# Loading order of the start, and the way one bank's operands are built, in a recurrent/attention decoder block

## The chip, the cores and the metric

The kernel runs on one core of a Trainium2 chip. A core has TensorE (PE, matrix products; its weight loads are listed as PEld), VectorE (DVE), ScalarE (ACT), GpSimd (POOL) and SyncE (SP). Every engine works through its own instructions in order. DMAs are issued here by SP and by ACT, each a queue in order: an issue that waits for a free buffer holds all issues behind it. The metric is device time in microseconds of one execution. A tile is named by its tag in the program (wraw, S, T, hf and so on), and the profile leaves buffer numbers out.

## The reference, cut to what matters

x is 2048 rows of 1024 float32 values, one layer.

```python
mod = c_act @ w_mod[l] + b_mod[l]              # c_act = silu(c), one row of 1024
shift, scale, gate = jnp.split(mod, 3, axis=-1)
h = rms_norm(x, g_norm[l]) * (1.0 + scale[:, None, :]) + shift[:, None, :]
proj = h @ w_in[l]                             # 1024 x 8192
x_rnn, z_rnn, q, k, v, z_attn, g_r, g_a = jnp.split(proj, IN_SPLITS, axis=-1)
...
x = x + gate[:, None, :] * (merged @ w_o[l])
```

Between the two parts quoted stand a recurrent branch (causal convolution, gated linear recurrence) and an attention branch with three dilated windows; both end in a product with a 1024 x 1024 matrix. The change touches only how `h` is made and how `v`, the first eighth of the projection that is computed, is multiplied out.

## The kernel before, in words

*Split products.* All large products keep float32 accuracy by splitting each operand into a high part (rounded, written by ACT: `hi_act`) and a low part (the operand minus the high part, written by POOL: `lo_pool`, or by VectorE: `lo_dve`). `mm3` (L149) then makes three matmuls: high by high, high by low, low by high.

*Banks and halves.* The 2048 positions are four banks of 512. The projection runs in two halves of two banks: `values_half(f, xs)` for the half f, then 28 Strassen products (`strassen`, L272) for all other columns of `w_in`. A Strassen product multiplies 2 x 2 blocks (the two banks by the two halves of the 1024 input channels) with seven block products instead of eight. Its right operands are the blocks of `h`: `B11` and `B21` (first bank of the half, channels 0 to 511 and 512 to 1023), `B22` (second bank, upper channels) and four block sums `T1` to `T4`. `B12` (second bank, lower channels) is needed for the values only. The seven products are taken in the order B11, T2, T3, T1, B21, T4, B22.

*The start.* Constants and the nine parameter rows are loaded by SP, transposed by PE (L462) and copied into `par` (L463). `x0`, the first bank of x, is loaded in two tiles of 1024 KB by SP (L386, `load_x`) and normalised (`norm_x`: squares on ACT, scaling on VectorE, L396). Then come four groups j of 256 channels (L478 to L501). For shift and scale each, a group loads a tile of modulation weights (1024 KB, SP, L483). VectorE sums the products of its first KV = 6 channel blocks with `ca` = silu(c) into `acc` (L485, L487); PE adds blocks 6 and 7 in one-column matmuls (`pg<-ca,T`) and folds `acc` down with `ones` (`pg<-ones,acc`). The bias goes on at L498 (`mod`), and `gs` is made at L499. Then `build_even` builds the blocks k = 2j and 2j + 1 of the first bank. When all modulation weights are loaded, `x1`, the second bank, is loaded.

*build* (L398) makes one block of 128 channels by 512 positions: four PE transposes (L403), the high part by ACT out of PSUM (L407), the full value `hf` by VectorE out of PSUM (L408), and the low part, by VectorE where k is 0, 3 or 6 and by POOL otherwise.

*Values.* `load_wv(m)` brings the value weights of two heads, m = 0 to 3: four loads of 256 KB into `wraw` (five buffers, L350), each split by ACT (L155) and POOL (L161) into tiles `S` (seven buffers, four to one m). `values` makes two groups of 48 matmuls for each m and bank, with `h` as the stationary operand and 256 columns of weights moving; `store_values` copies the result out of PSUM on ACT (L549) and stores it from SP (L551). For m = 0 of the first bank, `values_by_halves` takes the lower channels first, so that it can start before the upper blocks are built. One half has 768 value matmuls.

*build_odd* (L419) is a generator that `values_half` steps once after each group of 48 matmuls: 6 steps during the first bank's m = 1 to 3, the rest during the second bank's m = 3, 0, 1, 2, up to 14 in all. In each of its first four steps it builds block k of `B12` and of `B22` and makes block k of `T1`, `T2` and `T3` (L436 to L439, splits at L441: T1 and T3 low on VectorE, T2 low on POOL). In its next four steps it makes `T4` out of the stored high and low parts of B21 and T2 (L447, L448; low on POOL).

*What sets the order.* Outside the attention part, a planner orders the instructions of each engine by the program's order and by its own model of the times; `tc.issue_after(ins)` holds the issues of a block behind one instruction of the same engine. There are 14 buffers `T` of 8 KB a partition: x0 takes 2, B11 and B21 4, the modulation weights 8; x1, B22 and the block sums take them over as they come free.

## Time and profile before

| | us |
|---|---|
| three runs | 2361.22, 2364.11, 2366.56 (median 2364.11) |
| profiled execution | 2364.77, its span 2363.0 |
| start, 0 to 32.7 | no value matmul yet |
| values of the first half, 32.7 to 160.3 | 127.6 |
| Strassen products of the first half, 160.3 to 786.8 | 626.5 |
| values of the second half, 786.8 to 896.2 | 109.4 |
| Strassen products of the second half, attention, output | the rest, 1466.8 |

A row of a group of instructions reads: line, engine, operation, output<-input, shape, count | total busy time in us, mean of one in ns | idle time of the engine just before them, and what ended it. A row of a list in order of time reads: start, duration, engine, line, operation. A row of the waits reads: who waited <- for whom: total us, times, longest. A row of busy times by stage reads: stage, its length, then busy us (and count) of PE, PEld, DVE, ACT, POOL, then the granted clock of TensorE, the share of DMA time and GB/s.

### The profile page before, as it was taken

What the parts mean: (1) busy time and instruction counts of PE and PEld (TensorE: products, weight loads), DVE (VectorE), ACT (ScalarE), POOL (GpSimd) and SP (SyncE); (2) the same over time, 40 slices, a digit from 0 to 9 for tenths busy, and PEclk for the clock granted to TensorE, in tenths of its full rate; (3) what the DMA queues carried; (4) which work ended last, traced back from release to release, by engine and by line L of the source; (5) the groups of instructions that cost most, each with busy time, mean ns of one, the idle gap of its engine ahead of it and who ended that gap; (6) DMA issues with size and microseconds to landing.
All of it is one profiled execution on the core that took longest, in us unless ns stands there. A gap on an engine that the chain in (4) does not pass through costs nothing.

```text
span 2363.0 us, 34030 instructions
## 1 busy us (share of the span) xinstructions
PE 2232.6 (94%) x11397; PEld 1877.8 (79%) x11397; DVE 1340.2 (57%) x2423; ACT 1170.4 (50%) x2332; POOL 1003.8 (42%) x765
## 2 busy tenths in 40 slices
PE   5999999999999989999999998799999999989998
PEld 5897777777777888888888877688888898978887
DVE  6847666666575653544444462266666777645433
ACT  3436656666642434655444410366667878622111
POOL 2566656665555553433121110355445656443000
PEclk9999999999999999999999999899999999999999
DMA  7266777777788639999776776888999889797652
GB/s 266 82 207 235 267 240 259 255 248 249 251 272 251 205 120 322 326 346 314 247 243 231 222 264 212 259 262 255 300 299 273 263 248 287 217 337 275 225 178 97
DMA packets 420902, 585.44 MB, mean 248 GB/s; under 512 B 72446, under 2 KB 278518, under 8 KB 419704
## 3 DMA queue, kind: packets, MB, share of 16 engines
q1 hardware_dynamic: 383288, 463.72, 62.9%
q10 hardware_dynamic: 37440, 119.55, 13.3%
q8 instruction: 90, 1.47, 0.2%
q14 instruction: 84, 0.69, 0.1%
HBM read 367.14 MB, written 216.01 MB: 247 GB/s over the span
## 4 chain that ended last, share of the span: by engine, by line
PE 61%; DMA 12%; DVE 11%; ACT 5%; issue 5%; POOL 3%; SPq 2%; ACTq 1%; DVEq 0%; POOLq 0%
PE pj L147 43%; PE pq L147 7%; PE o L147 3%; PE sc L147 3%; PE pg L147 2%; DMA wraw<-in_w_in_dram 2%; POOL S L161 1%; PE pT L1082 1%; DMA w<-wD 1%; DVE acc L487 1%; DMA wD<-s 1%; ACT S L188 1%; DMA kraw<-qT 1%; PE pT L1095 1%; DMA qT<-t 1%
## 5 line engine op out<-in xcount | busy, mean ns | idle before, releaser
L147 PE MATMUL pj<-T,S 128*128 128x512 f32 x4704 | 1119.5, 398 | 33.7 <-DVE ev L340 15.7
L147 PEld LDWEIGHTS pj<-T,S 128*128 128x128 f32 x4704 | 887.8, 189 | 254.0 <-DVE ev L340 21.1
L147 PE MATMUL pj<-yh,w 128*128 128x512 f32 x1024 | 371.7, 408 | 11.7 <-ACT yh L155 10.4
L161 POOL TENSOR_TENSOR S<-wraw,S 128x512 fp32r<-128x512 f32 x168 | 240.7, 1444 | 175.8 <-ACT S L188 100.5
L147 PEld LDWEIGHTS pj<-yh,w 128*128 128x128 f32 x1024 | 195.6, 191 | 50.3 <-ACT yh L155 12.5
L147 PE MATMUL pj<-yl,w 128*128 128x512 f32 x512 | 204.0, 399 | 2.3 <-POOL yl L161 1.4
L998 ACT ACTIVATE pp<-pp,st 128x256 f32<-128x256 f32 (+3 forms) x256 | 133.8, 524 | 89.5 <-DVE st L997 88.7
L147 PE MATMUL pj<-S,T 128*128 128x256 f32 x1152 | 161.9, 297 | 10.3 <-POOL S L161 7.0
L147 PEld LDWEIGHTS pj<-S,T 128*128 128x128 f32 x1152 | 151.9, 202 | 12.3 <-POOL S L161 8.0
L161 POOL TENSOR_TENSOR S<-s,S 128x512 fp32r<-128x512 f32 x84 | 114.7, 1366 | 89.7 <-ACT S L188 43.7
L164 DVE TENSOR_TENSOR ptl<-pT,pth 128x384 fp32r<-128x384 f32 (+1 forms) x160 | 97.8, 628 | 60.8 <-ACT pth L155 58.6
L1062 ACT ACTIVATE pp<-pp,M 128x256 f32<-128x256 f32 (+3 forms) x256 | 118.0, 523 | 12.7 <-DVE M L1186 12.7
L642 DVE SCALAR_TENSOR_TENSOR xc<-xr,par,xc 128x512 f32<-128x512 f32 x96 | 87.0, 907 | 61.2 <-ACT xc L636 58.1
L997 DVE CUSTOM_DVE_ANT_0 pp<-sc,msk 128x256 f32<-128x256 f32 (+3 forms) x256 | 105.2, 449 | 24.6 <-PE sc L147 21.4
L294 DVE TENSOR_TENSOR u<-pj,u 128x512 f32<-128x512 f32 x56 | 38.4, 686 | 140.8 <-PE pj L147 91.1
L147 PEld LDWEIGHTS pj<-yl,w 128*128 128x128 f32 x512 | 98.1, 192 | 18.5 <-POOL yl L161 2.6
L161 POOL TENSOR_TENSOR kq<-kraw,kq 128x512 fp32r<-128x512 f32 (+1 forms) x64 | 100.4, 1578 | 19.4 <-ACT kq L155 13.9
L161 POOL TENSOR_TENSOR vh<-vraw,vh 128x256 fp32r<-128x256 f32 (+1 forms) x64 | 66.4, 1037 | 94.8 <-ACT vh L155 83.1
L161 POOL TENSOR_TENSOR wh<-vraw,wh 128x640 fp32r<-128x640 f32 (+1 forms) x32 | 48.4, 1513 | 135.2 <-ACT wh L155 74.7
L147 PE MATMUL pq<-oh,mh 128*128 128x512 f32 x256 | 98.0, 394 | 7.9 <-ACT mh L155 7.9
L147 PE MATMUL pq<-ol,mh 128*128 128x512 f32 x256 | 100.8, 394 | 0.3 <-POOL ol L161 0.3
L147 PE MATMUL pq<-oh,ml 128*128 128x512 f32 x256 | 99.6, 390 | 0.0
(290 smaller groups left out, 3886.2 us busy)
## 6 DMA issues: line engine op xcount, KB each, us to landing
sD<-S ACTq DMA_DIRECT2D x196, 512.0 KB, 3.1
S<-sD SPq DMA_DIRECT2D x196, 512.0 KB, 5.4
w<-wD SPq DMA_DIRECT2D x128, 512.0 KB, 6.2
wraw<-in_w_in_dram SPq DMA_DIRECT2D x136, 256.0 KB, 3.3
wD<-s ACTq DMA_DIRECT2D x64, 256.0 KB, 4.1
T<-in_w_mod_dram SPq DMA_DIRECT2D x8, 1024.0 KB
vN<-ev SPq DMA_DIRECT2D x64, 128.0 KB, 2.5
zaT<-ev SPq DMA_DIRECT2D x32, 256.0 KB, 2.8
```

Source lines behind the costliest of these rows:

```text
L147: last_mm[0] = nc.tensor.matmul(o, lhsT=l, rhs=r, start=st, stop=sp, **kw).ins
L161: nc.gpsimd.tensor_tensor(o, i, h.bitcast(F32), ALU.subtract)
L164: nc.vector.tensor_tensor(o, i, h.bitcast(F32), ALU.subtract)
L188: last_hi[0] = nc.scalar.activation(t[:, 0], src, AF.Copy).ins
L294: nc.vector.tensor_tensor(u2[:], Z[:], u1[:], ALU.add)
L487: nc.vector.scalar_tensor_tensor(acc[:], t[:, k, :], ca[:, k : k + 1], acc[:], ALU.mult, ALU.add)
L642: nc.vector.scalar_tensor_tensor(xc, xr[:, i : i + CH], cw(i), xc, ALU.mult, ALU.add)
L997: nc.vector.tensor_tensor_reduce(pdst, s_ps, mask, 1.0, 3e38, ALU.add, ALU.min, m_)
L998: nc.scalar.activation(pdst, pdst, AF.Exp, bias=m_, scale=-1.0, accum_out=l_)
L1062: nc.scalar.activation(pp, pp, AF.Copy, scale=w)
L1082: nc.tensor.transpose(pt[:, c0 + j * P : c0 + (j + 1) * P], pp[i][:, k * P : (k + 1) * P], ident)
L1095: nc.tensor.transpose(pt[:, c * P : (c + 1) * P], pp[:, half * P : (half + 1) * P], ident)
```

## The change

- *Start.* The two loads of `x0` are the first issues of SP. The constants are loaded by ACT's queue and the nine parameter rows by POOL's queue. Then SP loads the modulation weights of groups 0 and 1, the first half of value weights 0, groups 2 and 3, the second half of value weights 0, then `x1`, then value weights 1 (held behind x1 by `issue_after`). Before, SP loaded each group's modulation weights in the loop over the groups, and the value weights where the planner put them.
- *Modulation.* KV goes from 6 to 5: VectorE sums five channel blocks, PE takes three.
- *First bank (start only).* `hf` is made by ACT as a second pass over PSUM, and all low parts by VectorE. The first bank of the second half is built as before.
- *Second bank.* The eight blocks are built in the first four steps, with `hf` by ACT into eight buffers `hx` that are kept, and low parts on VectorE. The block sums take the next eight steps: T3 and T1 of block k in one, T2 and T4 in the next. T4 is B21 high - T2 (unsplit) + B21 low, two operations instead of three. All low parts are made by VectorE.

```diff
@@ -34,7 +34,7 @@
-KV = 6
+KV = 5
@@ -134,7 +134,6 @@
     pools = Pools()
 
     cs = T(cp, [P, N_CST_A], F32, "cs")
-    nc.sync.dma_start(cs[:], cst[:, :N_CST_A])
     ident = cs[:, K_ID : K_ID + P]
     qm = cs[:, K_QM : K_QM + 4]
     par = T(cp, [P, N_PAR], F32, "par")
@@ -189,7 +188,7 @@
         lo_pool(t[:, 1], src, t[:, 0])
         return t
 
-    pair_id, last_hi = {}, [None]
+    pair_id, last_hi, last_load = {}, [None], [None]
 
...
@@ -339,19 +338,21 @@
             else:
                 nc.vector.tensor_tensor(dst, perm(ps[:]), perm(u[:]), ALU.add)
 
+    def load_wv_half(m, k):
+
+        wh = T(wq, [P, KH, 2 * P], F32R, "S", bufs=7)
+        wl = T(wq, [P, KH, 2 * P], F32R, "S", bufs=7)
+        for k2 in range(0, KH, 2):
+            t = T(wq, [P, 2, 2 * P], F32, "wraw", bufs=NRAW)
+            rows = slice((k + k2) * P, (k + k2 + 2) * P)
+            last_load[0] = nc.sync.dma_start(
+                t[:], wcol(4 * D + m * 2 * P, 2 * P)[rows].rearrange("(k p) m -> p k m", p=P)).ins
+            hi_act(wh[:, k2 : k2 + 2], t[:])
+            lo_pool(wl[:, k2 : k2 + 2], t[:], wh[:, k2 : k2 + 2])
+        return wh, wl
+
     def load_wv(m):
-        ws = []
-        for k in range(0, KT, KH):
-            wh = T(wq, [P, KH, 2 * P], F32R, "S", bufs=7)
-            wl = T(wq, [P, KH, 2 * P], F32R, "S", bufs=7)
-            for k2 in range(0, KH, 2):
-                t = T(wq, [P, 2, 2 * P], F32, "wraw", bufs=NRAW)
-                rows = slice((k + k2) * P, (k + k2 + 2) * P)
-                nc.sync.dma_start(t[:], wcol(4 * D + m * 2 * P, 2 * P)[rows].rearrange("(k p) m -> p k m", p=P))
-                hi_act(wh[:, k2 : k2 + 2], t[:])
-                lo_pool(wl[:, k2 : k2 + 2], t[:], wh[:, k2 : k2 + 2])
-            ws.append((wh, wl))
-        return ws
+        return [load_wv_half(m, k) for k in range(0, KT, KH)]
 
...
@@ -383,7 +384,7 @@
         xs = []
         for r in range(0, 4, 2):
             t = T(pool, [P, 2, D], F32, tag, bufs=bufs)
-            nc.sync.dma_start(t[:], xv[n, r : r + 2].rearrange("r j d -> j r d"))
+            last_load[0] = nc.sync.dma_start(t[:], xv[n, r : r + 2].rearrange("r j d -> j r d")).ins
             xs += [t[:, 0, :], t[:, 1, :]]
         return xs
 
@@ -395,69 +396,79 @@
             rstd(ss)
             nc.vector.tensor_scalar(t, t, ss[:, 1:2], None, ALU.mult)
 
-    def build(st, names, xs, k):
+    def build(st, names, xs, k, first=False, keep=None):
 
         hh, hl = B[names[k // KH]]
         pt = T(pg, [P, 4, P], F32, "pg")
         for r in range(4):
             nc.tensor.transpose(pt[:, r, :], xs[r][:, k * P : (k + 1) * P], ident)
         pv = pt[:].rearrange("p r j -> p (r j)")
-        hf = T(st, [P, CH], F32, "hf", bufs=2)
         g, s = gs[:, k : k + 1], sh[:, k : k + 1]
         nc.scalar.activation(hh[:, k % KH, :], pv, AF.Identity, bias=s, scale=g)
-        nc.vector.tensor_scalar(hf[:], pv, g, s, ALU.mult, ALU.add)
-        (lo_dve if k % 3 == 0 else lo_pool)(hl[:, k % KH, :], hf[:], hh[:, k % KH, :])
-        return hf
+        if keep is not None or first:
+            hf = keep if keep is not None else T(st, [P, CH], F32, "hf", bufs=2)[:]
+            nc.scalar.activation(hf, pv, AF.Identity, bias=s, scale=g)
+            lo_dve(hl[:, k % KH, :], hf, hh[:, k % KH, :])
+        else:
+            hf = T(st, [P, CH], F32, "hf", bufs=2)
+            nc.vector.tensor_scalar(hf[:], pv, g, s, ALU.mult, ALU.add)
+            (lo_dve if k % 3 == 0 else lo_pool)(hl[:, k % KH, :], hf[:], hh[:, k % KH, :])
 
     def operand(name):
         B[name] = (slot(), slot())
 
-    def build_even(st, xs, ks=range(KT)):
+    def build_even(st, xs, ks=range(KT), first=False):
         for k in ks:
-            build(st, ("B11", "B21"), xs, k)
+            build(st, ("B11", "B21"), xs, k, first)
 
     def build_odd(st, xs):
 
         B["B12"] = (T(st, [P, KH, CH], F32R, "b12h"), T(st, [P, KH, CH], F32R, "b12l"))
-        for name in ("B22", "T1", "T2", "T3"):
-            operand(name)
+        operand("B22")
         f32 = lambda b, i, k: B[b][i][:, k, :].bitcast(F32)
         tt = nc.vector.tensor_tensor
-
-        def split(name, k, t, lo):
+        h = [T(st, [P, CH], F32, "hx", bufs=KT)[:] for _ in range(KT)]
+        for k in range(KH):
+            for k2 in (k, KH + k):
+                build(st, ("B12", "B22"), xs, k2, keep=h[k2])
+            yield
+        for name in ("T1", "T2", "T3", "T4"):
+            operand(name)
+
+        def split(name, k, t):
             hh, hl = B[name]
-            hi_act(hh[:, k, :], t[:])
-            lo(hl[:, k, :], t[:], hh[:, k, :])
+            hi_act(hh[:, k, :], t)
+            lo_dve(hl[:, k, :], t, hh[:, k, :])
 
         for k in range(KH):
-            h1 = build(st, ("B12", "B22"), xs, k)
-            h2 = build(st, ("B12", "B22"), xs, KH + k)
-            t = [T(st, [P, CH], F32, f"t{i}", bufs=1) for i in range(3)]
-            tt(t[0][:], h1[:], f32("B11", 0, k), ALU.subtract)
-            tt(t[0][:], t[0][:], f32("B11", 1, k), ALU.subtract)
-            tt(t[1][:], h2[:], t[0][:], ALU.subtract)
-            tt(t[2][:], h2[:], h1[:], ALU.subtract)
-            for i in range(3):
-                split(f"T{i + 1}", k, t[i], lo_pool if i % 2 else lo_dve)
+            h1, h2 = h[k], h[KH + k]
+            t = T(st, [P, CH], F32, "t0", bufs=2)[:]
+            tt(t, h2, h1, ALU.subtract)
+            split("T3", k, t)
+            tt(h1, h1, f32("B11", 0, k), ALU.subtract)
+            tt(h1, h1, f32("B11", 1, k), ALU.subtract)
+            split("T1", k, h1)
             yield
-        operand("T4")
-        for k in range(KH):
-            t = [T(st, [P, CH], F32, f"t{i}", bufs=1) for i in range(2)]
-            for i in range(2):
-                tt(t[i][:], f32("B21", i, k), f32("T2", i, k), ALU.subtract)
-            tt(t[0][:], t[0][:], t[1][:], ALU.add)
-            split("T4", k, t[0], lo_pool)
+            tt(h2, h2, h1, ALU.subtract)
+            split("T2", k, h2)
+            t = T(st, [P, CH], F32, "t0", bufs=2)[:]
+            tt(t, f32("B21", 0, k), h2, ALU.subtract)
+            tt(t, t, f32("B21", 1, k), ALU.add)
+            split("T4", k, t)
             yield
 
+
+    x0 = load_x(hp, 0, "T", 14)
+    nc.scalar.dma_start(cs[:], cst[:, :N_CST_A])
     prow = T(vx, [P, P], F32, "prow")
     for r0, ap in (
         (C_C, c[0]), (C_G, g_norm[0]), (C_BM, b_mod[0]), (C_BG, b_gate[0]), (C_CB, conv_b[0]), (C_LAM, lam[0]),
     ):
         n = ap.shape[0] // P
-        nc.sync.dma_start(prow[r0 : r0 + n, :], ap.rearrange("(k p) -> k p", p=P))
-    nc.sync.dma_start(prow[C_CW : C_CW + 32, :], conv_w[0].rearrange("j (k p) -> (j k) p", p=P))
-    nc.sync.dma_start(prow[C_BA : C_BA + 8, :], b_a[0])
-    nc.sync.dma_start(prow[C_BX : C_BX + 8, :], b_x[0])
+        nc.gpsimd.dma_start(prow[r0 : r0 + n, :], ap.rearrange("(k p) -> k p", p=P))
+    nc.gpsimd.dma_start(prow[C_CW : C_CW + 32, :], conv_w[0].rearrange("j (k p) -> (j k) p", p=P))
+    nc.gpsimd.dma_start(prow[C_BA : C_BA + 8, :], b_a[0])
+    nc.gpsimd.dma_start(prow[C_BX : C_BX + 8, :], b_x[0])
     pt = T(pg, [P, CH], F32, "pg")
     nc.tensor.transpose(pt[:, :N_PAR], prow[:N_PAR, :], ident[:N_PAR, :N_PAR])
     nc.vector.tensor_copy(par[:], pt[:, :N_PAR])
@@ -466,7 +477,6 @@
     nc.scalar.activation(ca[:], par[:, C_C : C_C + KT], AF.Sigmoid)
     nc.vector.tensor_tensor(ca[:], ca[:], par[:, C_C : C_C + KT], ALU.mult)
 
-    x0 = load_x(hp, 0, "T", 14)
     norm_x(vx, x0)
     operand("B11")
     operand("B21")
@@ -475,12 +485,23 @@
     mod = T(cp, [P, 2, KT], F32, "mod")
     sh = mod[:, 0, :]
     gs = T(cp, [P, KT], F32, "gs")
+    w_m, ws0 = {}, []
+
+    def load_mod(j):
+        for q in range(2):
+            w_m[q, j] = t = T(hp, [P, KT, 256], F32, "T", bufs=14)
+            c0 = q * D + j * 256
+            nc.sync.dma_start(t[:], w_mod[0, :, c0 : c0 + 256].rearrange("(k p) m -> p k m", p=P))
+
+    for j in range(4):
+        load_mod(j)
+        if j % 2:
+
+            ws0.append(load_wv_half(0, j // 2 * KH))
     for j in range(4):
         pm = T(pg, [P, 2, 2], F32, "pg")
         for q in range(2):
-            t = T(hp, [P, KT, 256], F32, "T", bufs=14)
-            c0 = q * D + j * 256
-            load = nc.sync.dma_start(t[:], w_mod[0, :, c0 : c0 + 256].rearrange("(k p) m -> p k m", p=P))
+            t = w_m[q, j]
             acc = T(vx, [P, 256], F32, "acc", bufs=2)
             nc.vector.tensor_scalar(acc[:], t[:, 0, :], ca[:, 0:1], None, ALU.mult)
             for k in range(1, KV):
@@ -498,8 +519,8 @@
         nc.vector.tensor_tensor(mod[:, :, j2], pm[:], bm[:, :, j2], ALU.add)
         nc.vector.scalar_tensor_tensor(gs[:, j2], mod[:, 1, j2], 1.0, par[:, C_G + 2 * j : C_G + 2 * j + 2],
                                        ALU.add, ALU.mult)
-        build_even(vx, x0, range(2 * j, 2 * j + 2))
-    with tc.issue_after(load.ins):
+        build_even(vx, x0, range(2 * j, 2 * j + 2), first=True)
+    with tc.issue_after(last_load[0]):
         x1 = load_x(hp, 1, "T", 14)
 
 
@@ -569,12 +590,16 @@
     def values_half(f, xs):
 
         n0, n1 = banks(f)
-        for _ in values_by_halves(vx, 0, load_wv(0), n0):
+        for _ in values_by_halves(vx, 0, load_wv(0) if f else ws0, n0):
             pass
         norm_x(vx, xs)
         odd = build_odd(vx, xs)
         for m in range(1, 4):
-            ws = load_wv(m)
+            if m == 1 and not f:
+                with tc.issue_after(last_load[0]):
+                    ws = load_wv(m)
+            else:
+                ws = load_wv(m)
             for _ in values(vx, m, ws, n0):
                 next(odd)
         for m in (3, 0, 1, 2):
```

## The prediction

> **What bounds the kernel now.** I read the page first, then busy times by stage, and inside the stages that the diff touches the order of time and the list of who waited for whom.
>
> ```profile
> span 2363.0 us, 34030 instructions
> PE 2232.6 (94%) x11397; PEld 1877.8 (79%) x11397; DVE 1340.2 (57%) x2423; ACT 1170.4 (50%) x2332; POOL 1003.8 (42%) x765
> PE 61%; DMA 12%; DVE 11%; ACT 5%; issue 5%; POOL 3%; SPq 2%; ACTq 1%; DVEq 0%; POOLq 0%
> ```
>
> ```profile
> 0.00:70.50 70.50, 41.39 (x235) 38.37 (x235) 49.20 (x126) 21.10 (x35) 17.99 (x18) 0.90 0.69 230
> 32.70:160.30 127.60, 119.14 (x897) 116.85 (x898) 87.65 (x132) 47.19 (x84) 62.76 (x44) 0.92 0.47 144
> 786.80:896.20 109.40, 100.13 (x801) 99.02 (x800) 57.00 (x79) 42.91 (x78) 59.88 (x42) 0.95 0.50 155
> ```
>
> The whole span is TensorE's: 94% busy, 61% of the chain. So a gain is only where PE idles or is slow, and the diff touches two such places: the first 160 us (start, and the values of the first half, 32.7 to 160.3), and 786.8 to 896.2 (the values of the second half). The columns after the length of a stage are PE, PEld, DVE, ACT, POOL. In the two value stages PE idles 127.6 - 119.1 = 8.5 us and 109.4 - 100.1 = 9.3 us; before 32.7 it hardly works. That is all that can be won except PE's own speed: some 24 us before the first value matmul, and 18 us in the stages.
>
> The start, in order of time (start, duration, engine; in square brackets the idle time before it and who ended it):
>
> ```profile
> 4.39 0.83 SPq L386 DMA_DIRECT2D T<-in_x_dram  x2
> 5.46 0.43 PE L462 MATMUL pg<-cs,prow 120*128 120x120 f32 x1 [5.46 <-DMA prow<-in_b_x_dram]
> 9.14 18.03 SPq L350 DMA_DIRECT2D wraw<-in_w_in_dram  x10
> 9.59 1.06 ACT L394 ACTIVATE hf<-T 128x1024 bf16<-128x1024 f32 x1 [1.61 <-DMA T<-in_x_dram]
> 15.22 0.99 PE L147 MATMUL pg<-ca,T 128*128 128x1 f32 x4 [9.33 <-DVE T L396]
> 27.21 5.40 SPq L483 DMA_DIRECT2D T<-in_w_mod_dram  x4
> 31.45 0.16 DVE L498 TENSOR_TENSOR mod<-pg,par 128x4 f32<-128x4 f32 x1 [1.96 <-PE pg L147]
> 32.73 5.95 PE L147 MATMUL pj<-S,T 128*128 128x256 f32 x24 [1.32 <-ACT T L407]
> 53.38 6.42 PE L147 MATMUL pj<-S,T 128*128 128x256 f32 x52
> 66.98 0.16 DVE L498 TENSOR_TENSOR mod<-pg,par 128x4 f32<-128x4 f32 x1 [1.56 <-PE pg L147]
> 70.50 8.75 PE L147 MATMUL pj<-S,T 128*128 128x256 f32 x63 [0.16 <-DVE T L164]
> ```
>
> SP is a queue in order. Ten value-weight loads (L350) hold it from 9.14 to 27.2, because they wait for free wraw tiles, and the modulation weights of groups 1 to 3 stand behind them. Group 0 gives its shift and scale at 31.45, group 3 at 66.98; only from 70.5 has PE both halves of the operand and streams. The two rows of value matmuls show a second thing: 24 take 5.95 us (0.248 each), 52 take 6.42 us (0.123 each). PE runs at half rate in part of the start, though the granted clock of the slice says 1.00 there.
>
> **The change part by part.**
>
> *x ahead, parameters off SP.* Ten small DMAs leave SP; x is issued at 0.74 instead of 4.39, 3.65 us earlier. x was there at 9.59, 5.2 us after its issue, so now at 5.9. The constants go to ACT's queue, one issue of some 0.4 us, beside an idle ACT: nothing. The nine parameter loads go to POOL's queue, which no DMA of this trace uses. Bounds: as on SP (nine landed by 5.46), and at POOL's nearest row, 1.3 us per instruction (the s<-wraw row below), 9 x 1.3 = 11.7, plus some 2 us to land: 14. I take 12, nearer to the upper end, since it is POOL's own row. At 12 it costs nothing: the first modulation tile cannot be there before (next step). At 14 it costs 2 us. POOL has nothing else to do before the first split of weights. Waiting for these loads are PE's first transpose and DVE's copy of the parameters; behind it on DVE stand the scaling of x and the sums.
>
> The Trainium skill, SBUF — State Buffer, section "SBUF: two separate sides", speaks against this part: descriptors of a DMA that POOL issues are written through a port pair that VectorE can hold, so such loads starve. By that rule the loads would be late by VectorE's work before they land; the scalings of x, four of 0.75 us (L396, below), are 3 us, an end of 2351 instead of 2348. No run here shows it yet, and the sum does not need it.
>
> *Modulation weights ahead of the value weights.* The rate while DMA is the limit:
>
> ```profile
> 20.00:25.00 5.00, 1.30 (x5) 0.94 (x6) 5.00 (x4) 2.78 (x5) 5.00 (x4) 1.00 0.53 169
> 35.00:40.00 5.00, 5.00 (x31) 5.00 (x31) 4.75 (x9) 0.00 (x0) 0.97 (x1) 1.00 1.10 348
> ```
>
> 348 GB/s is 3.0 us for a tile of 1024 KB. x (two tiles) is done at 8.9, group 0 at 11.9 and 14.9, group 1 at 20.9, the first half of value weights 0 at 22.4, group 2 at 28.4, group 3 at 34.4, the second half at 35.9, x of the second bank at 41.9, value weights 1 (added wait: behind that x on SP) at 44.9. The dip to 169 GB/s at 20 to 25, SP blocked, goes. Weights 1 must be split by four POOL operations (1.46 each, S<-wraw below), so are ready at 51; PE wants them some 6 us after the operand is complete, so they cost nothing unless that comes before 45.
>
> Sums of group 0, with KV = 5: L485 and four L487,
>
> ```profile
> 31.91 1.44 ACT L407 ACTIVATE T<-pg,mod,gs 128x512 fp32r<-128x512 f32 x2 [5.79 <-DVE gs L499]
> 34.16 0.68 DVE L164 TENSOR_TENSOR T<-hf,T 128x512 fp32r<-128x512 f32 x1
> 38.48 0.58 PE L147 MATMUL pg<-ca,T 128*128 128x1 f32 x4
> 39.02 2.57 DVE L487 SCALAR_TENSOR_TENSOR acc<-T,ca,acc 128x256 f32<-128x256 f32 x5
> L147 PE MATMUL pg<-ca,T 128*128 128x1 f32 x64 | 12.6, 301 | 9.7 <-DVE T L396 9.3 <-DVE mod L498 0.4
> ```
>
> 0.51 us an operation alone (five in 2.57), so 2.4 per tile. Last tile at 14.9, sums at 17.3; I add 2 for x's scaling on the same engine; then the last matmuls at 0.25 each (four in 0.99), ten of them, 2.5; then the same 1.3 us from mod (31.45) to the first value matmul (32.73). 17.3 + 2 + 2.5 + 1.3 = 23.1, and the first half of the weights, split by ACT and POOL, is there at 23.3. So PE's dense work starts at 23.5 instead of 32.7: 9.2 us earlier.
>
> From there PE's own work counts, since it was busy for 119.1 of the 127.6 us. Groups 1 to 3: with KV = 5 the 64 matmuls of ca (two instructions each) become 96, 8 per group more, 24 here, at 0.25 (slow) or 0.145 (four in 0.58): 3.5 to 6, I take 5 of cost. The 8 operations that VectorE saves are hidden work. In build, hf goes to ACT (0.72 each, two in 1.44) and the five POOL lows go to VectorE: ACT is idle at 47 of 127.6 us, nothing; VectorE gives up 0.80 (L408, below) and takes 0.68, nothing.
>
> The waits of PE in this stage, 32.6 to 160.3 (total, times, longest):
>
> ```profile
> PE pj L147 <- ACT T L407: 2.6, 2, 1.3
> PE pg L147 <- DVE acc L487: 2.5, 4, 1.4
> PE pg L403 <- DVE hf L408: 1.9, 1, 1.9
> PE pj L147 <- POOL S L161: 1.7, 1, 1.7
> ```
>
> The sums, the hf wait and the wait on POOL's S go, as tiles are no longer late and POOL has fewer lows; the wait for the built operand (2.6) stays, and some wait for weights 1 or for the norm of the second bank's x comes. 8.5 becomes 5: 3.5 gained, with -2 and 7 as ends. At last the half rate: 24 + some 45 instructions at 0.248 instead of 0.123 cost 9 us after 32.7. With no late tiles PE's stream has fewer holes; I take 3 of the 9. First half: 9.2 - 5 + 3.5 + 3 = 10.7 us.
>
> *The odd operands.* The second half has the clean picture:
>
> ```profile
> PE pj L147 <- POOL S L161: 5.3, 2, 3.0
> PE pg L403 <- DVE hf L408: 2.9, 2, 1.8
> 805.19 0.55 PE L403 MATMUL pg<-cs,T 128*128 128x128 f32 x3 [1.11 <-DVE T L396]
> L161 POOL TENSOR_TENSOR S<-wraw,S 128x512 fp32r<-128x512 f32 x23 | 33.0, 1460 | 17.6 <-PE pj L147 9.6 <-issue 4.3 <-ACT S L155 3.3
> L161 POOL TENSOR_TENSOR T<-t,T 128x512 fp32r<-128x512 f32 x8 | 12.0, 1504 | 11.7 <-ACT T L155 11.7
> L161 POOL TENSOR_TENSOR s<-wraw,s 128x512 fp32r<-128x512 f32 x4 | 5.2, 1288 | 13.9 <-DMA wD<-s 12.2 <-ACT s L155 1.7
> L164 DVE TENSOR_TENSOR T<-t,T 128x512 fp32r<-128x512 f32 x8 | 8.2, 1030 | 0.1
> L408 DVE TENSOR_SCALAR hf<-pg,gs,mod 128x512 f32<-128x512 f32 x10 | 7.9, 804 | 4.2 <-ACT b12h L407 2.2 <-POOL T L161 2.0
> L164 DVE TENSOR_TENSOR b12l<-hf,b12h 128x512 fp32r<-128x512 f32 x2 | 3.6, 1777 | 0.0
> L396 DVE TENSOR_SCALAR T<-T,ss 128x1024 f32<-128x1024 f32 x4 | 2.9, 752 | 0.1
> L155 ACT ACTIVATE T<-t 128x512 fp32r<-128x512 f32 x16 | 10.0, 631 | 30.8 <-DVE t L448 10.8 <-DVE t L437 9.7 <-DVE t L439 8.3
> ```
>
> PE waits 5.3 us for POOL's S because POOL, in order, sits in front of block-sum lows that wait for ACT (11.7 us idle). With all lows of a half's block sums and second-bank values on VectorE, POOL has only S left: the 5.3 go. The 2.9 behind hf (L403): VectorE's hf sat behind sums, ACT makes it now, and the sums come only after all eight blocks; I take half. The norm (1.1) stays. 5.3 + 1.5 less 0.8 for ACT's queue, where 8 hf more and 16 highs stand ahead of S: 6 us, ends -1 and 9.3. VectorE's own count stays: eight hf and four of the T4 subtractions go, some ten lows come. Its operations take 0.68 alone and up to 1.77 beside POOL, which is now busy 15 us less.
>
> Sum: 10.7 + 6 = 16.7. The profiled execution took 2364.8 us (span 2363.0 and 1.8 around it), the median of the three runs is 2364.1; 2364.8 - 16.7 = 2348.
>
> **The rivals.** Everything here compares with a noise of 0.2%, 4.7 us, which is what a measurement of this kernel can tell.
>
> *PE is fast in the start.* If the denser stream keeps PE at 0.123 us a matmul, the whole 9 us of half rate goes, 6 more, and the idle of both stages falls by 3 more: 2339. For it: the 52 at 0.123 come inside a long stream. Against: the 24 at 0.248 were a stream of 6 us too.
> The Trainium skill, TensorE: Matmul & The Clock Gate, Part 1, gives a rule: the array is at half clock until about 3.4 us of sustained activity. By that rule this rival holds, at 2339 where the sum by rows gives 2348. The trace agrees only in part: 5.95 us of streaming at 32.73 stayed slow to its end.
>
> *The start does not move as far.* If the parameters land only after the first tiles, or PE finishes each group's matmuls behind 24 slow value matmuls, the 9.2 shrink to 3 and the half-rate gain is nil: 2364.8 - 7.7 = 2357. For it: PE is in order, and the slice from 35 to 40 has PE busy for all of its 5.00 us.
>
> *VectorE's block sums become the bound (slower).* All lows and sums are now one row on VectorE, each low waiting for ACT's high: 48 operations at p (24 lows; six subtractions or additions for each of four k), and 24 hand-offs of 0.8 (ACT's 0.63 and the way there and back). Between the normalised x and the second Strassen product, which reads T2, there are some 98 us in the first half (an estimate: x there at 41.9, some 12 for its norm, the values' end at 149.6, 3 for the first product) and 88 in the second (18 us into the stage, by the row at 805.19, to 3 us behind an end at 103). At p = 1.77 the row is 85 + 19 = 104: 6 and 16 us late, less 16.7 gained: 2370. It is slower only from p = 1.71 on. The T<-t row above has a mean of 1.03, b12l 1.78 in two operations, and POOL, beside which the long ones stand, does less: little chance.
>
> *The gain does not come through.* The idle time moves behind the values, to the first Strassen products waiting for their weights: about 2363.
>
> **How the numbers follow.** Forecast (2342 to 2354) 0.50; fast PE 0.19; a short start 0.16; no effect 0.07; VectorE bound 0.08. The likeliest is 2348. Leaving out the worst of the slow rival and the far end of the fast one (all ends together, 9.2 + 7 + 9 - 3.5 + 9.3 = 31, give 2334): 2331 to 2361. Below 2359.4 lie the first three but for 0.01 of the short start: 0.84; slower than 2368.8: 0.08; the rest 0.08.
>
> **What would show it.** The first value matmul near 23 us and PE's stream from about 60 (now 70.5); the four mod rows about 10 us apart; L350 no longer holding SP before the modulation weights; in both value stages no PE wait on POOL S; the first Strassen matmul near 150, and the second value stage near 103 us long. Wrong would be: PE waits on DVE T or ACT T at the first Strassen products, parameter loads landing after 15 us, or PE still at 0.25 us a matmul through most of the start.

## The result, and the profile after

The changed kernel is slower: ratio to the kernel before 1.0044, 95% interval 1.003 to 1.0058 (medians 2374.46 and 2363.65 us). 2348 was forecast, with 2331 to 2361 as the range. The profiled execution took 2371.3 us (span 2369.6), 6.6 us of span more than before.

Busy times by stage of the changed kernel (stage, length, then PE, PEld, DVE, ACT, POOL, granted clock, share of DMA, GB/s); the limits are the first value matmul and the first Strassen product of each half:

```profile
0.00:53.70 53.70, 14.03 (x63) 13.29 (x63) 19.53 (x85) 15.71 (x26) 10.08 (x18) 1.00 0.81 264
53.70:175.20 121.50, 118.75 (x900) 118.43 (x901) 60.91 (x111) 58.80 (x101) 42.76 (x28) 0.96 0.35 104
175.20:800.80 625.60, 590.14 (x2492) 469.38 (x2492) 409.74 (x492) 348.90 (x579) 373.99 (x265) 0.98 0.76 257
800.80:901.70 100.90, 97.57 (x807) 96.93 (x806) 46.04 (x81) 48.95 (x87) 44.08 (x29) 0.98 0.54 167
```

Before, the start was 32.7, the first value stage 127.6, the second 109.4 (110.0 by the limits used here). So both value stages became shorter, by 6 and 9 us, and the start became 21 us longer; the Strassen products between kept their length (626.5 before, 625.6 now). The loss is all in the start. Its instructions in order of time (rows left out are marked by dots):

```profile
1.30 0.70 POOL L468 DMA_DIRECT2D prow<-in_c_dram  x1 [0.46 <-issue]
...
6.21 1.06 ACT L395 ACTIVATE hf<-T 128x1024 bf16<-128x1024 f32 x1 [3.76 <-DMA T<-in_x_dram]
7.14 0.52 POOL L471 DMA_DIRECT2D prow<-in_b_x_dram  x1 [1.55 <-DMA prow<-in_c_dram]
...
12.20 0.46 PE L473 MATMUL pg<-cs,prow 120*128 120x120 f32 x1 [12.20 <-DMA prow<-in_b_x_dram]
...
15.18 0.28 DVE L474 COPY par<-pg 128x120 f32<-128x120 f32 x1
...
21.87 1.38 ACT L154 ACTIVATE S<-wraw 128x512 fp32r<-128x512 f32 x2 [8.97 <-DMA wraw<-in_w_in_dram]
...
35.43 1.32 ACT L154 ACTIVATE S<-wraw 128x512 fp32r<-128x512 f32 x2 [12.18 <-DMA wraw<-in_w_in_dram]
36.13 2.48 POOL L160 TENSOR_TENSOR S<-wraw,S 128x512 fp32r<-128x512 f32 x2 [11.06 <-DMA wraw<-in_w_in_dram]
36.77 1.28 ACT L477 ACT_TABLE_LOAD   x1
38.06 0.21 ACT L477 ACTIVATE ca<-par 128x8 f32<-128x8 f32 x1
...
38.70 1.44 PE L146 MATMUL pg<-ca,T 128*128 128x1 f32 x6 [26.04 <-DVE ca L478]
...
53.77 1.20 PE L146 MATMUL pj<-S,T 128*128 128x256 f32 x4
```

The parameters are in `par` at 15.46 (15.18 and 0.28). The next thing that the modulation needs is one ACT operation of 0.21 us, the sigmoid of c (L477). It runs at 38.06. ACT works in order, and in its list the sigmoid stands behind the four splits of value weights 0 (L154). The second two of them wait until 35.4 for weights that the new loading order brings behind all modulation weights. PE waits 26.0 us for `ca`, with the modulation weights of all groups there or on the way. This is 22.6 us of waiting (38.06 less 15.46) for an operation whose input was ready. In the kernel before, the same operation ran right behind the copy of the parameters, ahead of every split:

```profile
6.25 0.21 ACT L466 ACTIVATE ca<-par 128x8 f32<-128x8 f32 x1 [4.24 <-DVE par L463]
```

A smaller delay stands ahead of it: PE's transpose of the parameters ends at 12.66, but VectorE copies them into `par` only at 15.18, behind the scalings of x in its own list.

The second value stage, PE's waits and the groups that the forecast spoke of:

```profile
PE pj L146 <- POOL S L160: 3.1, 2, 2.7
PE pg L404 <- DVE T L397: 0.2, 1, 0.2
L160 POOL TENSOR_TENSOR S<-wraw,S 128x512 fp32r<-128x512 f32 x23 | 36.9, 1630 | 43.3 <-PE pj L146 42.5 <-POOL T L160 0.8
L163 DVE TENSOR_TENSOR T<-hx,T 128x512 fp32r<-128x512 f32 x12 | 9.8, 818 | 0.6 <-ACT hx L410 0.6
L163 DVE TENSOR_TENSOR T<-t,T 128x512 fp32r<-128x512 f32 x8 | 6.5, 817 | 2.0 <-ACT T L154 2.0
```

PE waited 9.3 us there before (5.3, 2.9 and 1.1), now 3.3. POOL, which sat 11.7 us in front of block-sum lows, now idles in front of its splits almost only until PE has freed an S buffer (42.5 of 43.3 us). VectorE's lows take 0.82 us on average.

### The profile page after: what moved, and what is told of

The parts are those of the page before. It is cut to its first block, busy times and chain, and to the rows that moved or that the text cites. A ratio compares the mean times of both kernels' runs of the same rounds, so it can differ in the third digit from the quotient of the medians.

```text
span 2369.6 us, 34107 instructions
## 1 busy us (share of the span) xinstructions
PE 2236.5 (94%) x11429; PEld 1883.4 (79%) x11429; DVE 1303.9 (55%) x2414; ACT 1188.8 (50%) x2358; POOL 967.9 (41%) x743
## 5 line engine op out<-in xcount | busy, mean ns | idle before, releaser
L146 PE MATMUL pj<-T,S 128*128 128x512 f32 x4704 | 1122.1, 398 | 32.5 <-DVE ev L339 17.3
L160 POOL TENSOR_TENSOR S<-wraw,S 128x512 fp32r<-128x512 f32 x168 | 249.6, 1497 | 286.1 <-ACT S L187 107.5
L146 PE MATMUL pj<-S,T 128*128 128x256 f32 x1152 | 156.8, 292 | 5.9 <-POOL S L160 5.9
L160 POOL TENSOR_TENSOR S<-s,S 128x512 fp32r<-128x512 f32 x84 | 114.1, 1358 | 89.3 <-ACT S L187 44.5
L293 DVE TENSOR_TENSOR u<-pj,u 128x512 f32<-128x512 f32 x56 | 38.4, 686 | 146.1 <-PE pj L146 86.0
L160 POOL TENSOR_TENSOR kq<-kraw,kq 128x512 fp32r<-128x512 f32 (+1 forms) x64 | 100.3, 1576 | 19.2 <-ACT kq L154 18.8
L160 POOL TENSOR_TENSOR vh<-vraw,vh 128x256 fp32r<-128x256 f32 (+1 forms) x64 | 66.4, 1038 | 94.5 <-ACT vh L154 71.3
L160 POOL TENSOR_TENSOR wh<-vraw,wh 128x640 fp32r<-128x640 f32 (+1 forms) x32 | 48.4, 1513 | 133.6 <-ACT wh L154 79.2
```

The costliest lines, as they stand in the source:

```text
L146: last_mm[0] = nc.tensor.matmul(o, lhsT=l, rhs=r, start=st, stop=sp, **kw).ins
L160: nc.gpsimd.tensor_tensor(o, i, h.bitcast(F32), ALU.subtract)
L293: nc.vector.tensor_tensor(u2[:], Z[:], u1[:], ALU.add)
```

## The experiments

Each kernel is compared with runs of the kernel before on the same chip. Three chips were used, so rows are to be compared by their ratios. "First value" is the start of the first value matmul, "end 1" the start of the first Strassen product, "second" the length of the second value stage, all from one profiled execution each, in us. The expectations speak of three theories for the loss: A, the place of the sigmoid in ACT's list; B, that the parameters arrive late by POOL's queue; C, PE's own slow work in the start, which KV = 5 makes longer.

| kernel | first value | end 1 | second | ratio to before (95%) |
|---|---|---|---|---|
| before | 32.7 | 160.3 | 110.0 | 1 |
| changed kernel | 53.8 | 175.2 | 100.9 | 1.0044 (1.003 to 1.0058) |
| odd operands alone | 32.5 | 155.4 | 101.1 | 0.996 (0.9945 to 0.9976) |
| start alone | 53.9 | 180.2 | 106.1 | 1.0106 (1.0088 to 1.0124) |
| sigmoid first on ACT | 38.4 | 153.8 | 100.9 | 0.996 (0.9946 to 0.9973) |
| splits in order | 38.1 | 153.7 | 101.7 | 0.9972 (0.9953 to 0.999) |
| parameters on SP | 35.3 | 150.9 | 100.8 | 0.9931 (0.9912 to 0.9951) |
| the same, sigmoid put back behind the splits | 56.0 | 171.4 | 102.5 | 1.0027 (1.0008 to 1.0046) |
| parameters on SP, first bank built as before | 35.5 | 154.0 | 101.6 | 0.9952 (0.9933 to 0.997) |
| parameters on SP, KV = 6 | 33.9 | 148.2 | 101.1 | 0.9915 (0.9896 to 0.9933) |
| parameters on SP, KV = 7 | 32.3 | 147.0 | 103.0 | 0.993 (0.9906 to 0.9953) |
| parameters on SP, small chain late | 30.3 | 146.9 | 99.3 | 0.9934 (0.9909 to 0.9959) |
| parameters on SP, small chain late, KV = 6 | 28.3 | 150.1 | 101.5 | 0.9918 (0.99 to 0.9936) |
| parameters on SP, splits in order, chain late, KV = 7 | 30.7 | 153.2 | 102.3 | 0.9941 (0.992 to 0.9963) |

The stages that no kernel changes, from the second value stage's end to the end of the span, took 1463 to 1476 us in these profiles. The Strassen products of the first half took 623 to 630. So a difference of a few microseconds between two rows can be seen in the stages, but not in the ratios.

**Which part loses.** The odd operands alone: `build` with its new argument `keep` and `build_odd` of the changed kernel, put into the kernel before.

```diff
-    def build(st, names, xs, k):
+    def build(st, names, xs, k, first=False, keep=None):
...
-        for name in ("B22", "T1", "T2", "T3"):
-            operand(name)
+        operand("B22")
...
+            for k2 in (k, KH + k):
+                build(st, ("B12", "B22"), xs, k2, keep=h[k2])
```

> The kernel before with the new way of building the second bank's operands alone (start, KV and first bank as before). In the changed kernel the second value stage is 9.2 us shorter (109.4 to 100.2). If that part stands by itself, it is so here too, and the first stage loses its wait on POOL S as well: 9 to 12 us less than before, 2352 to 2355 us. If the gain there hangs on the changed start (another order of the queues), the second stage stays at 109 and the time at 2364 us.

Measured 0.996, the second stage 101.1 us, the first 122.9 (127.5 before). In the second stage this part wins by itself what it wins in the changed kernel, 9 us. The two stages together are 13.5 us shorter, the whole by the ratio 9.5. The start alone is the opposite:

```diff
-        operand("B22")
+        for name in ("B22", "T1", "T2", "T3"):
+            operand(name)
...
-                build(st, ("B12", "B22"), xs, k2, keep=h[k2])
+            h1 = build(st, ("B12", "B22"), xs, k)
+            h2 = build(st, ("B12", "B22"), xs, KH + k)
```

> The changed kernel with the old way of building the second bank's operands (start, KV = 5 and first bank as changed). Theory A: the late sigmoid is still there, so the first value matmuls at about 54, some 21 us later than before, and the second value stage at 109: 2364 + 15 to 21, that is 2379 to 2385 us. If the odd part were what makes the changed kernel slower, this one would be faster than before: 2352 us or less.

Measured 1.0106, the first value matmul at 53.9. That is 25 us slower than before (1.06% of 2366). In the profiled execution the first value matmul is 21.2 us later and the span 21.4 us longer, so the loss is in the start. The changed kernel's 1.0044 is this loss less the gain of the odd operands, as far as the intervals can tell (1.06% less 0.4% is 0.66%, and 0.44% was measured). One thing is not explained: the second value stage, in which this kernel is as before, is 106.1 us here, 4 us shorter.

**What in the start.** First, ACT's splits of value weights 0 held behind the sigmoid, all else as in the changed kernel:

```diff
-    nc.scalar.activation(ca[:], par[:, C_C : C_C + KT], AF.Sigmoid)
+    ca_act = nc.scalar.activation(ca[:], par[:, C_C : C_C + KT], AF.Sigmoid).ins
...
-            ws0.append(load_wv_half(0, j // 2 * KH))
+            with tc.issue_after(ca_act):
+                ws0.append(load_wv_half(0, j // 2 * KH))
```

> Theory A (ACT's order): in the changed kernel the sigmoid of c stands on ACT behind the split of the second half of value weights 0, which lands at 35.4 us; so the modulation sums start at 38.7 although the parameters were there at 15.5. Here the splits are held behind the sigmoid. Then ca is ready near 15.5. But the build of group 0 still stands behind the same split on ACT, so its first high part comes at about 37 instead of 49.5: some 12.5 us less than the changed kernel, 2362 us. Theory B (arrival: the parameters come late by POOL's queue): they still land at 12.2, nothing changes, 2374 us. Theory C (PE's own slow work in the start, more matmuls with KV = 5): nothing changes beyond 2 us, 2372 us or more.

Measured 0.996, 2355.9 us, below all three theories. In order of time:

```profile
12.32 0.46 PE L473 MATMUL pg<-cs,prow 120*128 120x120 f32 x1 [12.32 <-DMA prow<-in_b_x_dram]
...
15.65 0.21 ACT L477 ACTIVATE ca<-par 128x8 f32<-128x8 f32 x1 [1.29 <-DVE par L474]
...
16.11 1.44 PE L146 MATMUL pg<-ca,T 128*128 128x1 f32 x6 [3.33 <-DVE ca L478]
...
25.12 0.87 DVE L509 SCALAR_TENSOR_TENSOR acc<-T,ca,acc 128x256 f32<-128x256 f32 x2
...
38.35 1.22 PE L146 MATMUL pj<-S,T 128*128 128x256 f32 x4
```

The parameters land as late as in the changed kernel (12.3), and the whole start moves 15 us forward, the end of the stage 21. Theory B is out as the cause of these 15 us, and so is C: PE has the same matmuls. Theory A forecast 2362. It had the place right (the first high part of group 0 is made at 37.5, behind the second split, about 37 expected), but too small a gain. In the changed kernel PE does most of group 1's modulation matmuls between the build of group 0 (49.5) and its first value matmul (53.8). Here it does them while the build waits. The value stage is another 6 us shorter: PE doesn't wait in it (2.75 us in the changed kernel), and its granted clock is 0.99 instead of 0.96.

Then the parameters by SP's queue behind x0, and nothing else:

```diff
-        nc.gpsimd.dma_start(prow[r0 : r0 + n, :], ap.rearrange("(k p) -> k p", p=P))
+        nc.sync.dma_start(prow[r0 : r0 + n, :], ap.rearrange("(k p) -> k p", p=P))
...
-    nc.gpsimd.dma_start(prow[C_BX : C_BX + 8, :], b_x[0])
+    nc.sync.dma_start(prow[C_BX : C_BX + 8, :], b_x[0])
```

> The parameter loads go on SP's queue, behind x0 and ahead of the modulation weights; all else as in the changed kernel. Theory A: the planner now puts the sigmoid of c ahead of both splits, and the group-0 build ahead of the second one; the first value matmuls move from 53.7 to about 27 and the whole gets about 23 us shorter than the changed kernel, 2351 us. Theory B: only the earlier landing counts, 12.2 to about 6, so 6 us, 2368 us. Theory C: nothing beyond 2 us, 2372 us.

Measured 0.9931, 16 us below before (2366.3 x 0.0069). The time is what theory A expected (2351), the start isn't: the first value matmul is at 35.3, and 27 was expected.

```profile
9.15 0.29 SPq L471 DMA_DIRECT2D prow<-in_b_x_dram  x1
...
10.94 0.43 PE L473 MATMUL pg<-cs,prow 120*128 120x120 f32 x1 [10.94 <-DMA prow<-in_b_x_dram]
...
13.45 0.21 ACT L477 ACTIVATE ca<-par 128x8 f32<-128x8 f32 x1
...
24.52 1.38 ACT L154 ACTIVATE S<-wraw 128x512 fp32r<-128x512 f32 x2 [6.31 <-DMA wraw<-in_w_in_dram]
```

The parameters are only 1.3 us earlier than by POOL's queue (10.9 against 12.2). But with another queue for them the planner wrote ACT's list in another order: the sigmoid ahead of the splits. Whether it is the queue or the order is told apart by the next kernel, the same with the sigmoid (and the product that makes `ca` of it) put back behind both splits:

```diff
-    nc.scalar.activation(ca[:], par[:, C_C : C_C + KT], AF.Sigmoid)
...
+    with tc.issue_after(last_split[0]):
+        nc.scalar.activation(ca[:], par[:, C_C : C_C + KT], AF.Sigmoid)
```

> The changed kernel with the parameters on SP (0.9931 of before), and the sigmoid of c put back behind both splits of value weights 0 on ACT. Theory A: that one place in ACT's order brings the whole loss back, first value matmul near 51 to 54 us, 1.002 to 1.004 of before. Theory B (POOL's queue, not the order): the parameters still land near 11, so it stays at 0.993 to 0.995.

Measured 1.0027, the first value matmul at 56.0.

```profile
25.04 1.40 ACT L352 ACTIVATE S<-wraw 128x512 fp32r<-128x512 f32 x2 [9.78 <-DMA wraw<-in_w_in_dram]
38.57 1.34 ACT L352 ACTIVATE S<-wraw 128x512 fp32r<-128x512 f32 x2 [12.13 <-DMA wraw<-in_w_in_dram]
39.93 1.28 ACT L501 ACT_TABLE_LOAD   x1
41.22 0.21 ACT L501 ACTIVATE ca<-par 128x8 f32<-128x8 f32 x1
```

With the parameters on SP and one 0.21 us operation moved back in ACT's list, the loss is there again. So the order on ACT is the cause: set by hand, it takes the first value matmul from 53.8 to 38.4 with the loads on POOL, and from 35.3 to 56.0 with them on SP. Between the two kernels with the sigmoid ahead 3 us remain (38.4 and 35.3); no run divides them between the queue and the rest of the planner's order. Why the planner took the other order (it may have expected the parameters later by POOL's queue) no profile shows.

**What is left of the start.** Parameters by POOL again, with both splits placed: the first behind the sigmoid, the second behind the build of group 1.

```diff
+        with tc.issue_after(after):
+            for i, t in enumerate(ts):
+                hi_act(wh[:, 2 * i : 2 * i + 2], t[:])
+                lo_pool(wl[:, 2 * i : 2 * i + 2], t[:], wh[:, 2 * i : 2 * i + 2])
...
+    split_raw(ws0[0], ca_act)
...
+        if j == 1:
+            split_raw(ws0[1], last_hf[0])
```

> The changed kernel, parameters still by POOL's queue, but the split of the first half of value weights 0 held behind the sigmoid of c on ACT, and that of the second half behind the build of group 1. Theory A (ACT's order is the whole loss): the group-0 build no longer waits for the weights that land at 35.4, so some 3 us less than with the first split alone held (which took 0.996 of before): 0.994 to 0.995 of before, about what the parameters on SP gave (0.9931). Theory B (POOL's queue itself costs): no better than 0.996, since the parameters still land at 12.2.

Measured 0.9972, no better than with the splits only behind the sigmoid; by the numbers this is what theory B expected. Its profile says otherwise:

```profile
21.95 1.38 ACT L154 ACTIVATE S<-wraw 128x512 fp32r<-128x512 f32 x2 [6.14 <-DMA wraw<-in_w_in_dram]
23.34 1.28 ACT L562 ACT_TABLE_LOAD   x1
24.63 0.21 ACT L562 ACTIVATE e<-e 128x8 f32<-128x8 f32 x1
...
24.88 0.30 DVE L563 TENSOR_SCALAR e<-e 128x8 f32<-128x8 f32 x1 [7.43 <-ACT e L562]
...
33.81 0.78 ACT L428 ACTIVATE T<-pg,mod,gs 128x512 fp32r<-128x512 f32 x1 [8.97 <-DVE gs L543]
...
36.80 1.42 PE L146 MATMUL pg<-ca,T 128*128 128x1 f32 x6
38.08 1.20 PE L146 MATMUL pj<-S,T 128*128 128x256 f32 x4
```

The second split is out of the way, and group 0 is built from 33.8 on instead of 37.5. That wins nothing, since PE has most of group 1's modulation matmuls ahead of its first value matmul and ends them only at 38. And the second split was not all that stands in ACT's list. The exponential of the softplus chain (L562), again an operation of 0.21 us on 8 columns, stands behind the first split, which waits for its weights until 21.95. VectorE is in order too: it stops at that chain's next operation for 7.43 us, and the rest of the chain and the sums of group 0 stand behind it. So this result need not speak for POOL's queue (here, too, the parameters are in `par` at 15.6): the trace shows the same mechanism with a second small operation. In the kernel with the sigmoid first the same wait stands on VectorE from 17.5 to 25. That this wait is what is left is read from the trace; no run takes the chain out of the way with the parameters on POOL.

**The small chain out of the way.** To the kernel with the parameters on SP, the softplus chain held behind group 3's scale:

```diff
-        nc.vector.scalar_tensor_tensor(gs[:, j2], mod[:, 1, j2], 1.0, par[:, C_G + 2 * j : C_G + 2 * j + 2],
-                                       ALU.add, ALU.mult)
+        last_gs = nc.vector.scalar_tensor_tensor(gs[:, j2], mod[:, 1, j2], 1.0, par[:, C_G + 2 * j : C_G + 2 * j + 2],
+                                       ALU.add, ALU.mult).ins
...
-    nc.vector.scalar_tensor_tensor(e1[:], la, -1.0, la, ALU.mult, ALU.min)
+    with tc.issue_after(last_gs):
+        nc.vector.scalar_tensor_tensor(e1[:], la, -1.0, la, ALU.mult, ALU.min)
```

> The changed kernel with the parameters on SP, and the chain of some 25 small VectorE operations (the softplus constants, L536 to L549) held behind the last group's gs. In the start with the parameters on SP, VectorE has waits and small operations of this chain between the sums of group 0 (18.8 to 29.3 us), and mod of group 0 comes at 30.3. If these hold up the start: mod at about 25 and 3 to 5 us less than without, 0.991 of before. If PE's cold matmuls set it anyway: no change, 0.993.

Measured 0.9934, as without this edit (0.9931). Group 0's shift and scale (`mod`) come 5 us earlier (25.3 instead of 30.3), end 1 is 4 us earlier (146.9). Between the first value matmul and end 1 PE has no idle time, as without this edit:

```profile
30.25:51.83 21.58, 21.58 (x118) 21.58 (x119) 14.42 (x29) 9.67 (x14) 5.93 (x5) 0.97 0.87 299
51.83:146.89 95.06, 95.06 (x782) 95.06 (x782) 57.06 (x110) 51.68 (x91) 35.29 (x26) 0.97 0.40 119
```

4 us of 2348 are 0.17%, less than half of the interval's width (0.5%), so the ratio neither confirms nor denies this gain; the stages do show it.

**Sums on VectorE or on PE.** Of a group's eight channel blocks, KV are summed on VectorE. To the kernel with the parameters on SP:

```diff
-KV = 5
+KV = 7
```

> The changed kernel with the parameters on SP and KV = 7 instead of 5: VectorE sums seven channel blocks, PE takes one. It takes 64 one-column instructions of about 0.24 us from PE (15 us) and gives VectorE 16 operations of 0.48 (8 us). Theory C, as what is left of the start (PE, slow, sets the pace of 9 us from group to group): groups come 6 to 7 us apart and the whole is 8 to 12 us shorter than with KV = 5, 0.989 of before. If VectorE sets the pace, no change or longer: 0.993 or more.

Measured 0.993. End 1 is again 4 us earlier (147.0), but the first three groups still come 9 us apart (`mod` at 30.4, 39.4, 48.9 and 54.5): what PE saved, VectorE took, which was busy for 20.7 of the 22.2 us between first value matmul and fourth `mod` (12.0 of 21.5 with KV = 5). With KV = 5 VectorE waits for PE's sums ahead of three of the four `mod`, with KV = 7 only ahead of the last. With KV = 6:

```diff
-KV = 5
+KV = 6
```

> The changed kernel with the parameters on SP and KV = 6. With KV = 7 the groups came at 30.4, 39.4, 48.9, 54.5 us against 30.3, 39.7, 48.9, 56.8 with KV = 5, and the first value stage ended 4 us sooner, but the whole was not shorter beyond its uncertainty. Between the two: end of the first value stage at 147 to 151 us, 0.992 to 0.994 of before. PE's one-column matmuls as the pace would give 8 us a group; VectorE as the pace 9 us as now.

Measured 0.9915 (0.9896 to 0.9933), 2344.7 us, the lowest of all, by the ratio 20 us faster than the kernel before, and some 1.3% faster than the changed one (0.9915 against 1.0044). That 6 is better than 5 isn't shown: the intervals overlap, and end 1 differs by 2.7 us.

**All together.** Splits in order, parameters on SP, chain late, KV = 7:

```diff
-KV = 5
+KV = 7
...
+    split_raw(ws0[0], ca_act)
...
+        if j == 1:
+            split_raw(ws0[1], last_hf[0])
...
+    with tc.issue_after(last_gs):
+        nc.vector.scalar_tensor_tensor(e1[:], la, -1.0, la, ALU.mult, ALU.min)
```

> All together: parameters on SP, splits of value weights 0 held as in the run with the splits in order, the small chain late, KV = 7. If the effects add: 0.993 less 0.004 (KV) less 0.002 (chain): 0.987 of before, 2333 to 2337 us. If PE's or VectorE's work in the start is the floor: 0.990.

Measured 0.9941, no better than one of them (0.987 was expected if the effects added). The groups' `mod` are early (25.5, 36.4, 47.1, 52.7), but PE's waits from there to end 1 at 153.2 are new; the longest:

```profile
PE pg L425 <- DVE ss L173: 3.7, 1, 3.7
PE pj L146 <- ACT T L428: 1.3, 1, 1.3
```

The norm of the second bank's x (ss) is late now. The kernel with the parameters on SP and only the chain late had neither wait. The last one is the chain late with KV = 6, the parameters again on SP:

```diff
-KV = 5
+KV = 6
...
+    with tc.issue_after(last_gs):
+        nc.vector.scalar_tensor_tensor(e1[:], la, -1.0, la, ALU.mult, ALU.min)
```

> Parameters on SP, the small chain on VectorE held behind the last group, KV = 6: the candidate for the best. With KV = 5 the late chain ended the first value stage at 146.9 us instead of 150.9. KV = 6 takes 16 slow instructions of 0.24 from PE per half of the start: end at 143 to 147 us, 0.990 to 0.993 of before.

Measured 0.9918. The first value matmul is at 28.3, the earliest of all, and yet end 1 is at 150.1 (143 to 147 expected), since from the fourth `mod` on PE waits 5.1 us:

```profile
PE pj L146 <- POOL S L160: 3.3, 2, 2.9
PE pg L404 <- issue: 1.2, 1, 1.2
PE pg L404 <- DVE T L397: 0.6, 1, 0.6
```

So of the five starts that are earlier than 35, these two give back all or most of what they gained at another thing that is late (x's norm, or POOL's S). The other three keep all or most of it (end 1 at 146.9 to 148.2 instead of 150.9). Which of the five is the fastest as a whole can't be told: their ratios lie within 0.003 of each other, and each interval is wider.

**The first bank's new order.** In the kernel with the parameters on SP, the first bank's operands built as before the change:

```diff
-        build_even(vx, x0, range(2 * j, 2 * j + 2), first=True)
+        build_even(vx, x0, range(2 * j, 2 * j + 2))
```

> The changed kernel with the parameters on SP, and the first bank of the start built as before (hf on VectorE, five of eight low parts on POOL). The prediction took that part of the change as worth nothing: the first value stage within 2 us of 115.6 and the groups about 9 us apart, 0.993 to 0.994 of before. If POOL's low parts held VectorE's sums as they did in the kernel before (operations of 1.4 us for 0.5), groups come 10 us or more apart and the time is 4 us longer, 0.995.

Measured 0.9952 (0.9933 to 0.997), against 0.9931 (0.9912 to 0.9951) with it. End 1 is 3 us later (154.0), and PE waits 2.8 us for POOL's S (L160) where it waited for nothing. The time is what the second of the two expectations gave, but not for its reason: the groups come 9.8, 9.0 and 6.8 us apart, hardly slower than with the new order (9.4, 9.2, 7.9). So this part is worth about 3 us in the stage, where the prediction put it at nothing; the ratios agree with that but don't exclude zero.

## Why the prediction was wrong

**The step that failed** is group 0's: "Last tile at 14.9, sums at 17.3 ... So PE's dense work starts at 23.5", and with it "I take 12 ... At 12 it costs nothing". The landing came as forecast, 12 taken and 12.20 measured, but by luck: an issue on POOL took 0.51 to 0.70 us and not 1.3, and from the last issue to the first use it took 5.1 us and not 2. The rule of the Trainium skill (SBUF — State Buffer, section "SBUF: two separate sides"), that VectorE in some of its operations keeps POOL from writing the descriptors of such loads, is hardly tested here: by SP's queue they landed at 10.9, by POOL's at 12.2, and of VectorE's 3 us of scalings only 1.2 ran before that (from 11.00 on). I also took `ca` to be ready when its input was. Between the two is one ACT operation, and I looked on PE and VectorE only for what waits for the parameters. On ACT the sigmoid stood behind the splits of the first value weights, whose loads the same change puts behind the modulation weights (second half at 35.9 by my own list, measured 35.4). So I had the number by which the sigmoid was late, and took the first half of the splits as "there at 23.3", as if the second half held up nothing. This cost 15 us by the kernel with the sigmoid first (53.8 to 38.4), and 21 us by the pair with the parameters on SP (35.3, and 56.0 with the sigmoid put back).

**What the loads did** was right: x issued at 0.74 and used from 6.2 (5.9 forecast), the halves of value weights 0 used from 21.9 and 35.4 (there at 22.4 and 35.9 by the list). The four `mod` rows are 9.4, 9.2 and 7.9 us apart (about 10 forecast), and it is PE's matmuls that set this: VectorE waits 2.9, 1.3 and 3.9 us for them ahead of the last three. The bandwidth was not the mistake; the order of the consumers was.

**A size in the same step.** Even with the order mended, the first value matmul is at 35.3 and not at 23.5. My "ten" last matmuls "at 0.25 each, 2.5" was too few: in that kernel 26 matmuls of `ca` and `ones` of group 0 follow the first sums, from 23.05 to 28.7, 5.7 us. The sums ended late, those of the first tile at 22.9 and those of the last at 24.9 instead of 19.3. Ahead of them VectorE waited for ACT (norm of x and softplus chain, three waits of 1.35 us), and between them it did operations of the chain and scaled x. With the chain late they end at 19.5 and 21.8. From 28.7 to 30.3 PE waits for `mod`, which stands behind other sums and the chain on VectorE. The rest is PE's own order: the planner put most of group 1's matmuls (30.55 to 35.27) ahead of the first value matmul.

**The first value stage** was forecast at 126.1 (23.5 to 149.6) and took 121.5 in the changed kernel, 115.5 and 115.6 with the sigmoid ahead of the splits. Idle of PE 8.5 before, "becomes 5", measured 2.75, and none in the kernel with the parameters on SP. There PE's busy time fell as well, from 119.1 to 115.6, at a granted clock of 0.99 instead of 0.92; what moved the clock no run shows, and no term of the sum has it. The "24 here, at 0.25 or 0.145 ... I take 5 of cost" was right in the number of matmuls, and their cost lies partly ahead of this stage.

**The second value stage** was mis-sized by 3 us: 6 us forecast, 9 measured (110.0 to 100.9). PE's waits fell by the forecast 6, but by other parts than I had: the wait on POOL's S went from 5.3 to 3.1 instead of to zero, the hf wait of 2.9 went wholly, of which I had taken half, and the norm's went from 1.1 to 0.2. So POOL's place in front of block-sum lows explains 2.2 of the 5.3 us; what holds the rest no run shows (POOL's splits now wait mostly for S buffers that PE has not freed). The other 3 us are PE's busy time (100.8 to 97.6 within the same limits), at a granted clock of 0.98 instead of 0.95, and no term has them. The odd operands alone gave 0.996 (9.5 us), with 9.0 us in this stage and 4.6 in the first, of which the rest of the span took back a part.

**The sum.** With the order mended (parameters on SP) the change gives 0.9931, or 16.3 us (0.0069 of 2363.65), beside the 16.7 of my sum. That the two agree is luck, and no proof of the terms: the start, 9.2 us of the sum, lost 2.6 (35.3 for 32.7), and the value stages gained 12.0 and 9.2. These three make 18.6 us. The range's lower end, 2331, lies under the 2334 that all its far ends together give, and is worked out nowhere.

**The rivals.** None of the four held. VectorE did not become the bound: its block-sum lows took 0.82 us on average where 1.71 would have decided. PE wasn't fast in the start: six one-column matmuls still took 1.42 us at 65.50. "The start does not move as far" had the right place, but neither the mechanism nor the sign. The chance for slower, 0.08, was all on VectorE's block sums. That the planner writes another engine's list anew when loads change places was in no rival.

## What to carry to other kernels

When loads change places, look in each engine's in-order list for small operations with early inputs that stand behind an operation fed by the load that is now last: here 0.21 us of work stood 22.6 us behind a split. Where a planner writes the lists, the order it writes is part of the change, and moving a load to another queue can change it on engines that never touch that load; fix the order that matters by hand (the sigmoid ahead of the splits), or check it in the trace. And measure the parts of a change apart: one part of this one won 0.4%, the other lost 1.1%, and with the sigmoid ahead of the splits both together won 0.3 to 0.7%.
